# The order of SyncE's loads and stores, and wider sums of the samples' state, in a hybrid mLSTM and attention step

## The chip, the cores and the metric

The kernel runs on one core of one Trainium2 chip. The time is the device time of one launch in microseconds. The kernel before took 834.73 us, the median of three runs (834.29 to 835.82).

## The reference

One layer of a decoder with two branches, for a prompt of 1024 tokens and for eight samples of four tokens each. All numbers are 32-bit floats.

```python
h = rmsnorm(x, g_norm) * (1 + scale) + shift           # scale, shift, gate from silu(c) @ w_ada + b_ada
mq, mk, mv, mi, mf, mo, mz, aq, ak, av, az, gm, ga = split(h @ w_in)
y_m, C, n, m = mlstm(mq, mk, mv, mi, mf, mo, mz, C0, n0, m0)   # 4 heads of 128, chunks of 128
o   = sliding-window attention with sinks (8 heads, 2 key heads, window 128)
y_a = o * silu(az)
u   = sigmoid(gm) * (y_m @ w_mo) + sigmoid(ga) * (y_a @ w_ao)
y   = rmsnorm(x + gate * (u @ w_o), g_final)
```

For the samples, a head of the mLSTM starts from a given state `C0`, `n0`, `m0`:

```python
num = s @ v + w_inter * (q @ C);  dot = sum(s) + w_inter * (q @ n)
h   = num / max(|dot|, exp(-m_hat))
h   = h * rsqrt(mean(h * h) + eps) * g_mn
```

Outputs are `y` of prompt and samples, the new states `C`, `n`, `m` of both, and the last 128 keys and values.

## The kernel before

The tokens lie in the columns (1024 of the prompt and 32 of the samples), the channels in the partitions. Products in full precision are made of three products of rounded parts (a high and a low part of each operand). Weights come in tiles of 128 x 4 x 128 (`wr_...`, from a set of nine buffers), are rounded by ScalarE (`wh_...`), and VectorE takes the rest (`wl_...`). Most other tiles come from one set of 50 buffers (`ht`).

In order of time there are: the loads of the inputs, the norms and the scale and shift; the first two jobs (`ak`, `av`); jobs for the queries of the attention (`aq`) and for the first head's `mq`, `mk`, `mv`; then 18 pairs of jobs (`block_products`), each with seven products of blocks in place of eight. A product of a pair is twelve passes over 512 columns. The products of a pair are named by number: 5, 6, 2, 7, then product 1 of the next pair, then 3 and 4. At product 5 the pair calls `load()` of the next pair, which asks for its four tiles of weights. After product 2 stand small products for the samples (`smp`) of the next pair, which read all four tiles. Then follow the two output projections of the branches, and the last projection in row blocks (`foX` to `foZ`).

Between these products the attention, the heads of the mLSTM, the samples and the preparation of `w_out` run as generators ("streams"). A planner (`Side`) counts the time that the products should take (`side.now`) and decides between which products a generator's next step is emitted; a step yields how long it wants to wait until its next one. So a head (`head`) loads `hq`, `hk`, `hv`, `et`, `qw` in `load`, right behind the `U` products of `stage_b`, and uses them in `prep` a step later. `store` puts a store on a list, and it is emitted when 8 us of the planner's time are over, or when a load from the same memory comes.

All instructions then go through a scheduler that places them by the order of emission and by when its own model thinks them ready. TensorE's order is fixed to that of the emission (`in_order`). VectorE's and ScalarE's is fixed only while `V.on` and `S.on` are true: at the start, up to the line `V.on = S.on = False` behind the first two jobs, and in the last projection. SyncE's queue has no order of its own, except for loads with `late`. An edge of the kind `NoSync` orders two instructions in that plan; it makes no semaphore and no wait on the chip.

`sample_head(h)` computes the state of the samples for one head. The products with the old state are spread over four groups of 32 rows, and for every two heads `st` sums these groups with a matrix of zeros and ones (`C_S32`, 32 columns of the constants `cst`, 104 columns before their end), into rows 0 to 31 of a bank. ScalarE copies that to `sz`, it is scaled, transposed (`sty`), and multiplied by `gmn` into `gs`. This happens twice, for heads 1 and 3.

Of the kernel before, what the change touches and what calls it, by code (L numbers as in the profile page):

```python
# [15 lines left out]
ALU = mybir.AluOpType  # L16
# [8 lines left out]
NS = NB * NT  # L25
# [11 lines left out]
C_ID, C_S9, C_TRI, C_CM, C_AM, C_TS, C_CS, C_RS, C_S32, C_BM, C_S64 = 0, 128, 137, 265, 393, 649, 681, 713, 745, 777, 785  # L37
C_END = 849
# [135 lines left out]
def body(tc, a):  # L174
    nc = tc.nc
    with ExitStack() as ctx:
# [11 lines left out]
        def pb(shape, name):  # L188
            return ps.tile(shape, F32, tag="b", bufs=2, name=name)

        def po(shape, name):
            return ps.tile(shape, F32, tag="o", bufs=2, name=name)

        def ht(shape, name, dt=F32):
            return sp.tile(shape, dt, tag="half", bufs=50, name=name)

        def sm(shape, name, bufs=3, dt=F32):
            return sp.tile(shape, dt, tag=name, bufs=bufs, name=name)

        last = {}  # L200

        def no_sync(ins, others):
            for o in others:
                tc.add_manual_dep(ins, o.name, mybir.DependencyInfo(
                    mybir.DependencyClass.NoSync, mybir.DependencyReason.DATA), reason="order of the work")

        def in_order(ins, eng="PE"):
            i = getattr(ins, "ins", ins)
            no_sync(i, [last[eng]] if eng in last else [])
            last[eng] = i  # L210
# [27 lines left out]
        V, S, G = Ordered(nc.vector, "V"), Ordered(nc.scalar, "S"), Ordered(nc.gpsimd, "G")  # L238
# [8 lines left out]
        def stores(src=None):  # L247

            for e in list(due):
                if e[0] <= side.now or (src is not None and e[1].tensor is src):  # L250
                    due.remove(e)
                    issue(*e[1:])

        def dma(out, in_, late=False):
            stores(in_.tensor)
            issue(out, in_, late)

        def issue(out, in_, late=False, eng=None):
            ins = (eng or nc.sync).dma_start(out, in_)  # L259
            ins = getattr(ins, "ins", ins)  # L260
            if late:
                no_sync(ins, free)
                free.clear()
            free.append(ins)

        side = Side(stores, {"m": (2, 35.0), "a": (5,8.0), "x": (2, 0.0), "s": (1, 0.0), "g": (1, 0.0)}, 1.5)
        def mm(out, lhsT, rhs, start, stop, share=1, more=False):
            n = int(np.prod(rhs.shape[1:]))
            side.now += max(n, 250) / 2400 if rhs.dtype == F32R else max(n * 4 // share, 128) / 2400
            side.products += 1  # L270
            in_order(nc.tensor.matmul(out, lhsT, rhs, start=start, stop=stop, skip_group_check=more))  # L271

        def tr(out, in_, idn):
            side.now += 0.11
            side.products += 1
            in_order(nc.tensor.transpose(out, in_, idn))  # L276
# [38 lines left out]
        load_x(0, 0, 2, xT[0])  # L315
        small = ht([128, 512], "small")
        issue(small, a["small"])
        load_x(0, 2, KT, xT[0])
        load_x(1, 0, KT, xT[1])
        cst = cp.tile([128, C_END], F32, name="cst")  # L320
# [3 lines left out]
        ident = cst[:, C_ID:C_ID + 128]  # L324
# [4 lines left out]
        gmn, bada, gnorm = vec[:, 0:4], vec[:, 4:20], vec[:, 20:28]  # L329
# [656 lines left out]
        gs = cp.tile([128, NH, NS], F32, name="gs")  # L986
# [51 lines left out]
        def head(h):  # L1038
# [128 lines left out]
            if h == 2:  # L1167
                at["n0"], at["n1"] = (cp.tile([128, NH, NB], F32, name=n) for n in ("n0", "n1"))
                dma(at["n0"], a["state_n"])
                for i in range(NH):  # L1170
                    side.add("s", sample_head(i), "ob")
# [3 lines left out]
        def sample_head(h):  # L1175
            an, sxb, fls, wes = st["an"], st["sxb"], st["fls"], st["wes"]
            z = ht([128, 512], "sz")
# [28 lines left out]
            for b, m in zip(bs, ns_):  # L1206
                vf, vm = ht([NS, 512], f"vf{h}"), ht([96, 512], f"vm{h}", F32R)
                w = m * 129 + m % 2
# [31 lines left out]
                return  # L1240
            yield 3.0, "o"
            tot = po([128, 2, 129], f"st{h}")
            for i, (_, n4) in enumerate(tails):
                mm(tot[:NS, i], cst[:, C_S32:C_S32 + NS], n4, start=True, stop=True)
            ns = z[:NS, 0:258].rearrange("p (m e) -> p m e", e=129)
            S.copy(ns, tot[:NS])
            ssq = sm([NS, 2], "sssq", 2)
            for i in range(2):
                jk = sm([128, 128], "mjk", 2, BF16)
# [6 lines left out]
            for i in range(2):  # L1256
                V.tensor_scalar(ns[:, i, 0:128], ns[:, i, 0:128], d[:, i:i + 1], r[:, i:i + 1], op0=ALU.mult, op1=ALU.mult)
            yield 4.0, "b"
            ty = pb([128, 2, NS], f"sty{h}")
            for i, (g, _) in enumerate(tails):  # L1260
                tr(ty[:, i], ns[:, i, 0:128], ident[:NS, :NS])
                V.tensor_scalar(gs[:, g], ty[:, i], gmn[:, g:g + 1], None, op0=ALU.mult)
                samples_done.append(g)
            tails.clear()
            if h == NH - 1:
# [1108 lines left out]
```

## Time and profile before

| what | us |
|---|---|
| median of three runs | 834.73 |
| profiled execution | 832.12 |
| its span | 830.4 |
| TensorE busy | 810.4 |
| VectorE busy | 593.8 |
| ScalarE busy | 420.5 |
| GpSimd busy | 67.2 |

The profile is of one execution. Its span goes from the first instruction to the last, and the execution's time has 1.72 us more around it. Starts of products are measured and their ends are modelled, so the distance from one start to the next says more of a product's cost than its own duration. A row of the timeline has the start, the duration, engine, line, operation, the tiles written and read, the shape of the array and the sizes; in brackets stands the idle time before it and who ended it. SPq is SyncE's queue of DMA issues: a row there is the issue, and the data land later.

### The profile page before, as it was taken

What the parts mean: (1) busy time and instruction counts of PE and PEld (TensorE: products, weight loads), DVE (VectorE), ACT (ScalarE), POOL (GpSimd) and SP (SyncE); (2) the same over time, 40 slices, a digit from 0 to 9 for tenths busy, and PEclk for the clock granted to TensorE, in tenths of its full rate; (3) what the DMA queues carried; (4) which work ended last, traced back from release to release, by engine and by line L of the source; (5) the groups of instructions that cost most, each with busy time, mean ns of one, the idle gap of its engine ahead of it and who ended that gap; (6) DMA issues with size and microseconds to landing.
All of it is one profiled execution on the core that took longest, in us unless ns stands there. A gap on an engine that the chain in (4) does not pass through costs nothing. (4 is left out here: it accounts for less than half of the span.)

```text
span 830.4 us, 15038 instructions
## 1 busy us (share of the span) xinstructions
PE 810.4 (98%) x5129; PEld 669.3 (81%) x5129; DVE 593.8 (72%) x1479; ACT 420.5 (51%) x1030; POOL 67.2 (8%) x128
## 2 busy tenths in 40 slices
PE   6999999999999999999899999999999999999996
PEld 3779897888788788888788877887888789997775
DVE  4889886656656456475577785897569988974776
ACT  5664365555474564555455453544346654334343
POOL 0120000000000001000001000000002104250000
PEclk9999999999999999999999999999999999999998
DMA  9997766356436425479856345464336785643633
GB/s 334 378 357 238 184 201 213 118 150 217 143 111 189 114 85 150 140 240 286 268 188 205 120 141 155 143 203 142 103 117 196 230 288 172 212 146 122 202 109 108
DMA packets 106689, 153.96 MB, mean 185 GB/s; under 512 B 20448, under 2 KB 54368, under 8 KB 106580
## 3 DMA queue, kind: packets, MB, share of 16 engines
q1 hardware_dynamic: 100964, 142.25, 54.1%
q10 hardware_dynamic: 4176, 6.56, 2.2%
q0 software_dynamic: 1472, 4.20, 1.4%
q8 instruction: 40, 0.66, 0.3%
q14 instruction: 37, 0.30, 0.1%
HBM read 109.22 MB, written 44.75 MB: 185 GB/s over the span
## 5 line engine op out<-in xcount | busy, mean ns | idle before, releaser
L220 ACT ACTIVATE p<-p,nmx 128x256 f32<-128x256 f32 (+1 forms) x64 | 31.0, 486 | 12.4 <-DVE nmx L220 12.1
L271 PE MATMUL g_aq<-h_h,wh_aq 128*128 128x384 f32 (+1 forms) x96 | 32.2, 336 | 0.0
L271 PE MATMUL g_aq<-h_h,wl_aq 128*128 128x384 f32 (+1 forms) x96 | 30.9, 322 | 0.0
L271 PE MATMUL g_aq<-h_l,wh_aq 128*128 128x384 f32 (+1 forms) x96 | 30.8, 321 | 0.0
L271 PE MATMUL g_w_mo<-ym_l,wh_w_mo 128*128 128x384 f32 (+1 forms) x96 | 30.8, 321 | 0.0
L271 PE MATMUL g_w_mo<-ym_h,wh_w_mo 128*128 128x384 f32 (+1 forms) x96 | 30.8, 321 | 0.0
L271 PE MATMUL g_w_mo<-ym_l,wl_w_mo 128*128 128x384 f32 (+1 forms) x96 | 30.8, 321 | 0.0
L220 DVE CUSTOM_DVE_ANT_0 p<-sc,cst,sink 128x256 f32<-128x256 f32 (+1 forms) x64 | 26.2, 464 | 5.3 <-PE sc L271 5.2
L259 POOL DMA_DIRECT2D oD<-uqv x16 | 8.9, 554 | 183.2 <-ACT uqv L220 161.0
L220 DVE COPY p<-pt 128x512 f32<-128x512 f32 (+1 forms) x16 | 10.5, 657 | 13.6 <-PE pt L276 13.6
L271 PEld LDWEIGHTS g_aq<-h_h,wh_aq 128*128 128x128 f32 x96 | 18.0, 188 | 2.5 <-issue 1.5
L271 PEld LDWEIGHTS g_w_mo<-ym_l,wh_w_mo 128*128 128x128 f32 x96 | 18.0, 188 | 0.0
L271 PEld LDWEIGHTS g_aq<-h_l,wh_aq 128*128 128x128 f32 x96 | 18.1, 188 | 0.0
L271 PEld LDWEIGHTS g_w_mo<-ym_h,wh_w_mo 128*128 128x128 f32 x96 | 18.0, 188 | 0.0
L271 PE MATMUL sc<-ukv,uqv 64*128 64x256 f32 (+1 forms) x128 | 18.0, 390 | 0.0
L271 PEld LDWEIGHTS g_aq<-h_h,wl_aq 128*128 128x128 f32 x96 | 18.0, 188 | 0.0
L271 PEld LDWEIGHTS g_w_mo<-ym_l,wl_w_mo 128*128 128x128 f32 x96 | 18.0, 188 | 0.0
L220 ACT ACTIVATE p<-p,den 128x256 f32<-128x256 f32 (+1 forms) x32 | 14.5, 491 | 5.7 <-DVE den L220 5.6
L220 ACT ACTIVATE sq<-rows_h 128x512 f32<-128x512 f32 (+2 forms) x14 | 8.2, 582 | 17.8 <-issue 12.0
L220 DVE TENSOR_TENSOR et<-et,S 128x384 f32<-128x384 f32 (+1 forms) x12 | 6.1, 510 | 15.4 <-PE S L271 12.7
L271 PE MATMUL g_mq<-h_h,wh_mq 128*128 128x384 f32 (+1 forms) x48 | 16.8, 349 | 0.3 <-ACT mk L220 0.3
L276 PE MATMUL pt<-cst,p 128*128 128x128 f32 x120 | 16.4, 277 | 0.5 <-DVE mx L220 0.5
(2073 smaller groups left out, 2841.4 us busy)
## 6 DMA issues: line engine op xcount, KB each, us to landing
x<-xT SPq DMA_DIRECT2D x16, 256.0 KB, 5.6
early_h<-w_ada SPq DMA_DIRECT2D x8, 512.0 KB, 9.0
adar_ga<-w_ada SPq DMA_DIRECT2D x16, 256.0 KB, 4.0
wr_ga<-w SPq DMA_DIRECT2D x16, 256.0 KB, 2.9
wr_gm<-w SPq DMA_DIRECT2D x16, 256.0 KB, 3.6
taD<-gt SPq DMA_DIRECT2D x16, 256.0 KB, 2.2
tmD<-gt SPq DMA_DIRECT2D x16, 256.0 KB, 5.3
wor<-w_out SPq DMA_DIRECT2D x16, 256.0 KB, 5.1
```

Of the source, the lines that this page charges most:

```text
L220: ins = f(*args, **kw)
L259: ins = (eng or nc.sync).dma_start(out, in_)
L271: in_order(nc.tensor.matmul(out, lhsT, rhs, start=start, stop=stop, skip_group_check=more))
L276: in_order(nc.tensor.transpose(out, in_, idn))
```

## The change

Two edits. In `issue`, each load or store of SyncE that is emitted while the order of VectorE is not fixed gets an edge for the order behind the product that was emitted last. In `sample_head`, the sums `st` take all 104 columns of the constants from `C_S32` on, where they took 32; the copy takes the 104 rows; the two transposes take 104 rows and are both emitted ahead of the two multiplications, and their bank has room for 128 columns each. Rows and columns beyond 32 aren't used.

```diff
         def issue(out, in_, late=False, eng=None):
             ins = (eng or nc.sync).dma_start(out, in_)
             ins = getattr(ins, "ins", ins)
+            if eng is None and not V.on:
+                no_sync(ins, [last["PE"]])
             if late:
                 no_sync(ins, free)
                 free.clear()
...
             tot = po([128, 2, 129], f"st{h}")
+            w = C_END - C_S32
             for i, (_, n4) in enumerate(tails):
-                mm(tot[:NS, i], cst[:, C_S32:C_S32 + NS], n4, start=True, stop=True)
-            ns = z[:NS, 0:258].rearrange("p (m e) -> p m e", e=129)
-            S.copy(ns, tot[:NS])
+                mm(tot[:w, i], cst[:, C_S32:C_END], n4, start=True, stop=True)
+            nw = z[:, 0:258].rearrange("p (m e) -> p m e", e=129)
+            S.copy(nw[:w], tot[:w])
+            ns = nw[:NS]
...
-            ty = pb([128, 2, NS], f"sty{h}")
+            ty = pb([128, 2, 128], f"sty{h}")
+            for i in range(2):
+                tr(ty[:, i, 0:w], nw[:w, i, 0:128], ident[:w, :w])
             for i, (g, _) in enumerate(tails):
-                tr(ty[:, i], ns[:, i, 0:128], ident[:NS, :NS])
-                V.tensor_scalar(gs[:, g], ty[:, i], gmn[:, g:g + 1], None, op0=ALU.mult)
+                V.tensor_scalar(gs[:, g], ty[:, i, 0:NS], gmn[:, g:g + 1], None, op0=ALU.mult)
                 samples_done.append(g)
```

## The prediction

> **What bounds the kernel now.** I read the page first, then the waits of TensorE, then the timeline around the few places where TensorE stands still, then SyncE's own queue.
>
> ```profile
> span 830.4 us, 15038 instructions
> PE 810.4 (98%) x5129; PEld 669.3 (81%) x5129; DVE 593.8 (72%) x1479; ACT 420.5 (51%) x1030; POOL 67.2 (8%) x128
> PE xc L271 <- ACT xsq L220: 6.2, 1, 6.2
> PE S L271 <- DVE C L220: 2.3, 1, 2.3
> PE sty L276 <- DVE gs L220: 1.1, 2, 0.8
> ...
> PE bw L271 <- ACT bw L220: 0.7, 1, 0.7
> PE pt L276 <- DVE mx L220: 0.5, 1, 0.5
> PE g_mq L271 <- ACT mk L220: 0.3, 1, 0.3
> ...
> 818.00:830.40 12.40, 5.21 (x40) 4.84 (x39) 6.70 (x20) 3.00 (x9) 0.00 (x0) 0.81 0.23 85
> ```
>
> The first two lines are the page: TensorE is busy 810.4 of 830.4 us. Then come waits of TensorE: one of 6.2 us while the inputs arrive, and after that only small ones. The last line is one row of the table by stage: in the final 12.4 us TensorE works 5.2, so about 7 us are the closing chain of the last row block. Head and tail together are 13 of the 20 idle us, and the change reaches neither: its new line acts only while the flag of VectorE's ordering is off, which is from the end of the input projections of the first two jobs to the start of the final row blocks. No TensorE wait names a DMA. So in the middle the time is the sum of the products' pitches plus a few microseconds of stalls, and a change of the DMA order can only win those stalls or add new ones.
>
> **The wider state sums.** These are the fixed part. First the visit of `st`, in the timeline of TensorE, then two kinds of product without a change of array shape.
>
> ```profile
> L271 PE MATMUL st<-sz,cst x8: 273/273/298, 503.4 to 564.5; 128*32 128x129 f32 x8
> 503.05 0.39 PE L271 MATMUL bw<-t2h,wl_pgate__5971 128*128 128x512 f32 x1
> 503.37 0.63 PE L271 MATMUL st<-sz,cst 128*32 128x129 f32 x4
> ...
> 504.50 0.40 PE L271 MATMUL bw<-t2h,wl_pgate__5971 128*128 128x512 f32 x1
> ...
> 402.49 0.39 PE L271 MATMUL bw<-t2h,wl_pgate__4793 128*128 128x512 f32 x1
> 402.72 0.38 PE L271 MATMUL n<-hv,et 128*128 128x129 f32 x2
> 402.94 0.39 PE L271 MATMUL n<-C,qw 128*128 128x129 f32 x2
> 404.05 0.38 PE L276 MATMUL tk<-cst,hk 128*128 128x128 f32 x2
> 404.27 0.38 PE L276 MATMUL tv<-cst,hv 128*128 128x128 f32 x2
> ```
>
> From a start to the next start, a 512-column `bw` takes 402.72 - 402.49 = 0.23 us, two passes over 129 columns take 402.94 - 402.72 = 0.22, so 0.11 each, and two transposes take 404.27 - 404.05 = 0.22. Around `st`, 504.50 - 503.05 = 1.45 us hold the four passes of `st` and three `bw` (the one at 503.05 and two that lie between the second and third row, left out here). Less 3 x 0.23 that is 0.76 us for a visit. In the 128*128 shape, four passes at 0.11 would be 0.44. So a visit wins 0.32 us, and the first row shows eight passes in all, so there are two visits: 0.64 us. The loss is at the borders, where the array goes from 128*128 to 128*32 and back. 104 columns no longer fit into a 32-column shape, so I expect the row to say 128*128.
>
> The transposes of the sums:
>
> ```profile
> 516.14 0.39 PE L271 MATMUL bw<-h_h,wl_pgate__6128 128*128 128x512 f32 x1
> ...
> 517.04 0.24 PE L276 MATMUL sty<-cst,sz 32*128 32x32 f32 x1 [0.35 <-DVE gs L220]
> ...
> 517.78 0.39 PE L271 MATMUL bw<-h_h,wl_pgate__6128 128*128 128x512 f32 x1
> ...
> 579.00 0.39 PE L271 MATMUL by<-t3h,wl_phead_gate__6816 128*128 128x512 f32 x1
> ...
> 580.33 0.24 PE L276 MATMUL sty<-cst,sz 32*128 32x32 f32 x1 [0.77 <-DVE gs L220]
> ...
> 581.09 0.40 PE L271 MATMUL bx<-h_h,wl_phead_gate__6839 128*128 128x512 f32 x1
> ```
>
> The second transpose waits each time for VectorE's `gs`, which reads the first one out of the same bank; in the second visit VectorE has a long sum in front of it. The first visit costs 517.78 - 516.14 - 0.69 = 0.95 us, the second 581.09 - 579.00 - 0.69 = 1.40. After the change both transposes stand ahead of both reads, and have the full shape: 0.22 us a visit. That wins 0.73 + 1.18 = 1.91. The sum of this part is 2.55 us, all on TensorE, which is the bound here, so it should arrive whole.
>
> What could eat it: the weights of `st` grow from 32 to 104 columns, and the copy out of PSUM from 32 to 104 partitions.
>
> ```profile
> L271 PEld LDWEIGHTS n<-hv,et x64: 186/192/192, 236.4 to 469.2; 128*128 128x128 f32 x64
> 404.25 0.48 ACT L220 COPY et<-n 128x387 f32<-128x387 f32 x1 [3.00 <-PE n L271]
> ```
>
> A load of 128 columns is shown with 192 ns and yet its products follow each other at 0.11 us, so loads of that width are covered by the products before them; I cost the wider load at nothing, and the first load of a visit at most at 0.19 (two visits: 0.38). The Trainium skill, "TensorE: Matmul & The Clock Gate", section "LDWEIGHTS (loading the stationary operand)", speaks against this edit: it has the load's time go with the columns, columns / 1.2 ns. By it, as an estimate, eight loads would grow by 60 ns each, 0.48 us if none were covered, and the part would win 2.07. The 192 ns beside the 0.11 us here speak against that. The copy in the second row has 128 partitions and 387 columns and takes 0.48 us; the new one has 104 and 258, so it is below that, on an engine that is 51% busy, and only the small sums of the same visit follow it. I cost it at nothing too.
>
> **The order of SyncE's queue.** The added line gives each load and store a place behind the product emitted last. It is an edge for the order only; SyncE gets no wait on TensorE. ScalarE's and GpSimd's own DMAs are not touched. What moves is which DMA stands before which in one queue that stops at each unmet wait.
>
> ```profile
> 66.29 0.36 SPq L259 DMA_DIRECT2D n<-state_n  x1
> ...
> 371.01 0.33 SPq L259 DMA_DIRECT2D wr_ga<-w  x1
> ...
> 393.77 0.42 SPq L259 DMA_DIRECT2D wr_gm<-w  x1
> 394.48 1.87 SPq L259 DMA_DIRECT2D woDp<-wor  x2
> 396.45 0.39 SPq L259 DMA_DIRECT2D taD<-gt  x1
> 397.51 0.32 SPq L259 DMA_DIRECT2D hq<-qD  x1
> ...
> 397.24 0.39 PE L271 MATMUL bz<-h_h,wh_pgate__4766 128*128 128x512 f32 x1
> 397.92 0.83 PE L271 MATMUL U<-hv,hk 128*128 128x129 f32 x6
> ...
> 404.91 0.56 DVE L220 TENSOR_TENSOR et<-et,cst 128x384 f32<-128x384 f32 x1 [2.33 <-DMA tmD<-gt]
> 406.11 0.56 DVE L220 TENSOR_TENSOR qw<-qw,hq 128x384 f32<-128x384 f32 x1 [0.64 <-DMA qw<-wid]
> 406.99 0.71 PE L271 MATMUL S<-hq,hk 128*128 128x128 f32 x4 [2.33 <-DVE C L220]
> ```
>
> The first row is the plainest case: the code asks for `state_n` at the end of the third head, and SyncE issues it at 66 us. The second is the usual one: the weights of a pair are asked for at product 5 of the pair before, here the `bz` of 397.24, and the first tile was issued 26 us ahead. Stores run ahead too: `store` holds them back for 8 us of the planner's clock, yet `taD` goes at 396.45, as soon as it is ready, and stands before the head's loads (`hq`, and behind it `hk`, `hv`, `et` and `qw`), which the code asks for right behind the `U` of 397.92.
>
> This costs something in one place only. VectorE waits 2.33 us for `et` and 0.64 for `qw`; behind them in its queue stands the sum `C` that frees a bank for `S`, and TensorE idles 2.33 us. With the change, `woDp` and `taD` go behind the head's loads, since their 8 us are not over at 397.9, and `wr_gm`, whose product is earlier, stays before them. SyncE was through with `wr_gm` at 394.2, so the loads can go up to 397.51 - 394.2 = 3.3 us earlier, more than the 2.97 us that VectorE waited. I take the 2.33 us as won; the bounds are nothing (a buffer that isn't free, or VectorE placed otherwise) and 2.33.
>
> The new order also changes the plan for VectorE and ScalarE, which in this stretch are placed by readiness, and hands out buffers otherwise. For that I have no row; the stalls of this kind that the kernel has now outside `S` and `sty` are single waits like `bw` at 0.7 us, so I charge one more of 0.7, with bounds from -1.5 (`bw`, `pt` and `g_mq` of the first fence go, 0.7 + 0.5 + 0.3) to the 7.0 us of the slow rival.
>
> **Sum.** -2.55 - 2.33 + 0.7 = -4.2 us. The profiled execution took 832.12 us, its span and 1.72 us around it; it would take 827.9. The median of the runs is 834.73, 2.6 above that execution, and I keep that distance: 830.5 us. With the bounds this case reaches from 834.73 - 2.55 - 2.33 - 1.5 = 828.3 to 831.9, where most of the 2.33 us is gone again.
>
> **Rivals.** *The order is hidden.* No TensorE wait names a DMA, and the `S` stall may stay or be replaced by an equal one. Then only the sums count: 834.73 - 2.55 = 832.2. For it speaks that all other waits are under 1 us.
>
> *The weights come late (slower).* Their 26 us of lead shrink. From product 5 to the small products of the next pair, which read all four tiles, lie three products of twelve passes, 36 x 0.23 = 8.3 us, and a tile must land and be rounded before.
>
> ```profile
> wr_gm<-w SPq DMA_DIRECT2D x16, 256.0 KB, 3.6
> wr_av<-w SPq DMA_DIRECT2D x2, 256.0 KB, 9.7
> ```
>
> A median landing of 3.6 us leaves room; that of the first stage, 9.7, does not. It decides from a landing of somewhat under 8.3 us, if SyncE doesn't run ahead at all. It will run ahead by up to the 8 us of the stores, because it has no wait on TensorE. But where it stops at a buffer or a store just ahead of the weights, ScalarE and VectorE stand behind a missing tile. Priced at the one such wait that is shown, 2.33 us, in three of the 17 pairs that are loaded so: 3 x 2.33 - 2.55 = +4.4, 839.2 us.
>
> *The sums win nothing*, because the array shape is not what costs there, and the order nothing either: 834.7.
>
> **From this the numbers.** Forecast 0.40, hidden order 0.25, late weights 0.26, nothing 0.09. A measurement of this kernel can tell about 0.2%, 1.67 us, from no change: 833.06 to 836.40. Faster are the forecast and nearly all of the hidden order (0.21 of 0.25): 0.61. Within the bound lie the case of nothing and what is left of the hidden order: 0.13. Slower is the case of late weights: 0.26. The forecast's own range is 828.3 to 831.9. A range for 8 in 10 takes it in, the hidden order, the case of nothing, and the lower half of the late weights: 828.3 to 839.2.
>
> **What would show it.** Right: `st` rows of 128*128 with the next `bw` about 0.44 us later than without them; both `sty` transposes back to back and no wait for `gs`; `state_n` issued after 400 us; the head's loads before the stores of the same moment, and no wait of TensorE at `S` over 1 us. Wrong: a wait of ScalarE or VectorE on `wr` tiles of over 2 us with TensorE idle behind it; new waits of TensorE that sum to more than 2.6 us; or `st` with the same 0.76 us a visit.

## The result: 836.1 us, slower where faster was forecast

The median of the changed kernel is 836.11 us (835.10 to 837.22, 20 runs), that of the kernel before on the same chip 834.13 us (831.28 to 835.82, 20 runs): a ratio of 1.0025, 95% interval 1.0017 to 1.0033. The forecast was 830.5 us. The profiled execution of the changed kernel took 837.22 us, the longest of its 20, its span and 1.82 us around it; that of the kernel before took 832.12. So the two profiles differ by 5.1 us, and the medians by 2.0; why those distances differ is told with the ninth experiment. One execution of experiment 8, the profiled one, ran at a granted clock of 0.85 and took 899.60 us; it is left out of that experiment's figures.

Two lines of the page after the change:

```profile
span 835.4 us, 15022 instructions
PE 810.8 (97%) x5129; PEld 669.8 (80%) x5129; DVE 588.4 (70%) x1479; ACT 417.9 (50%) x1030; POOL 66.6 (8%) x128
```

The waits of TensorE (its product and line, the releaser, us in total, times, longest; `...` stands for rows that are left out):

```profile
...
PE g_w_mo L273 <- DVE wl_w_mo L220: 3.6, 4, 1.2
PE by L273 <- DVE hg1z L220: 1.5, 1, 1.5
PE sc L273 <- DMA ukv<-kD: 0.7, 1, 0.7
...
PE az L273 <- DVE ym_h L220: 0.5, 1, 0.5
PE smp L273 <- DMA wr_gm<-w: 0.5, 2, 0.2
```

TensorE is as busy as before, 810.8 us against 810.4. The waits `S` and `sty` are gone. In their place stand four waits of the memory's output projection (`g_w_mo`, the rounded low part `wl_w_mo` of the weights, made by VectorE), one for `hg1z`, one for `ym_h`, and some for data (`ukv`, `wr_gm`, and 0.5 us for `wg` in a row that is left out).

TensorE runs the same 5129 products in the same order in both kernels, so each can be set beside its twin. Where the distance between the two grows or shrinks, the time was lost or won. Up to 383 us the changed kernel falls behind by 1.6 us, in parts of 0.36 (arrival of the inputs), 0.53 (`wg`) and 0.70 (`ukv`). Then come +1.26 at `smp` (385 us), -2.50 at `S`, +0.36 at `bx` behind `gt`, -2.6 at the state sums, +2.1 in 640 to 662 us (`hg1z` and `ym_h`), and +1.02, +1.44, +1.07 and +1.08 in the memory's output projection (712 to 735 us), 4.6 in all. These steps sum to 4.8 of the 5.1 us. The wait for `wg` is no mark of the change: experiments 1 and 10, where no load has the edge, have 0.2 and 0.5 us of it. That for `ukv` stands in six of the seven kernels whose loads have the edge at that place (0.2 to 0.7 us) and in no other.

**The state sums** did what was worked out. TensorE's timeline of the changed kernel:

```profile
503.89 0.39 PE L273 MATMUL bw<-t2h,wl_pgate__5971 128*128 128x512 f32 x1
504.12 0.60 PE L273 MATMUL st<-sz,cst 128*104 128x129 f32 x4
...
505.01 0.39 PE L273 MATMUL bw<-t2h,wl_pgate__5971 128*128 128x512 f32 x1
...
516.66 0.39 PE L273 MATMUL bw<-h_h,wl_pgate__6128 128*128 128x512 f32 x1
516.89 0.34 PE L278 MATMUL sty<-cst,sz 104*128 104x104 f32 x2
...
517.55 0.40 PE L273 MATMUL bw<-h_h,wl_pgate__6128 128*128 128x512 f32 x1
...
578.46 0.39 PE L273 MATMUL by<-t3h,wl_phead_gate__6816 128*128 128x512 f32 x1
578.69 0.34 PE L278 MATMUL sty<-cst,sz 104*128 104x104 f32 x2
...
579.35 0.40 PE L273 MATMUL bx<-h_h,wl_phead_gate__6839 128*128 128x512 f32 x1
```

Counted as in the prediction (three long products of 0.23 us lie in each stretch), a visit of `st` takes 505.01 - 503.89 - 0.69 = 0.43 us instead of 0.76, and each visit of `sty` 0.20 instead of 0.95 and 1.40, with no wait between its two transposes. That is 2 x 0.33 + 0.75 + 1.20 = 2.6 us.

**The new waits.** VectorE of the changed kernel around the first of the four (in brackets: idle time before, and what ended it), and the products that wait:

```profile
711.61 0.55 DVE L220 SCALAR_TENSOR_TENSOR tgw_mo<-tgw_mo,g_w_mo 128x384 f32<-128x384 f32 x1 [0.43 <-PE g_w_mo L273]
...
713.16 0.54 DVE L220 TENSOR_TENSOR u_h<-u_h,tgw_mo 128x384 f32<-128x384 f32 x1
713.63 0.68 DVE L220 TENSOR_TENSOR wl_w_mo<-wr_w_mo,wh_w_mo 128x512 fp32r<-128x512 f32 x1
...
714.36 0.45 PE L273 MATMUL g_w_mo<-ym_l,wl_w_mo 128*128 128x384 f32 x1 [0.86 <-DVE wl_w_mo L220]
...
695.84 0.62 ACT L220 CAST wh_w_mo<-wr_w_mo 128x512 fp32r<-128x512 f32 x1 [2.95 <-PE g_w_mo L273]
```

The products that wait here are the first of the fifth job. Its weights had been there for long: ScalarE made their high part, the fifth of eight such casts, at 695.84. VectorE makes the low part only at 713.63, and before that it idles 0.43 us for a product of TensorE: the rounding stands in its queue behind a sum of the job before (`tgw_mo`, the row of 711.61), which can't start until that job's product is done. In the kernel before the same rounding stood at another place:

```profile
707.32 0.44 DVE L220 SCALAR_TENSOR_TENSOR tgw_mo<-tgw_mo,g_w_mo 128x288 f32<-128x288 f32 x1
707.68 1.73 DVE L220 TENSOR_TENSOR wl_w_mo<-wr_w_mo,wh_w_mo 128x512 fp32r<-128x512 f32 x1
```

It started at 707.68, behind the last sum of the third job, where the changed kernel has it two sums later, behind the second of the fourth, and TensorE came to its first product with it at 712.93. That is the first reading of the result: not a transfer that came late, but an instruction of VectorE that was given a later place.

### The profile page after: what moved, and what is told of

It reads as the page before. It is cut to its first block, busy times and chain, and to the rows that moved or that the text cites. A ratio compares the mean times of both kernels' runs of the same rounds, so it can differ in the third digit from the quotient of the medians.

```text
span 835.4 us, 15022 instructions
## 1 busy us (share of the span) xinstructions
PE 810.8 (97%) x5129; PEld 669.8 (80%) x5129; DVE 588.4 (70%) x1479; ACT 417.9 (50%) x1030; POOL 66.6 (8%) x128
## 4 chain that ended last, share of the span: by engine, by line
PE 81%; issue 6%; DVE 5%; DMA 5%; ACT 2%; SPq 1%; POOL 0%; DVEq 0%; POOLq 0%; ACTq 0%
PE bx L273 10%; PE bw L273 10%; PE by L273 10%; PE g_w_mo L273 5%; PE bz L273 5%; PE g_mq L273 3%; PE g_aq L273 3%; PE foW L273 3%; PE foX L273 3%; PE foY L273 2%; PE smp L273 2%; PE sc L273 2%; PE oT L273 2%; PE foZ L273 2%; PE pt L278 2%
## 5 line engine op out<-in xcount | busy, mean ns | idle before, releaser
L220 DVE SCALAR_TENSOR_TENSOR tgw_mo<-tgw_mo,g_w_mo 128x384 f32<-128x384 f32 (+1 forms) x24 | 12.2, 516 | 10.7 <-PE g_w_mo L273 10.5
```

The costliest lines, as they stand in the source:

```text
L220: ins = f(*args, **kw)
```

## Experiments

Unless something else is said, each kernel starts from the changed one, and is compared with the kernel before on the same chip (medians there: 834.72 us for the first four, 834.53 for the next four, 834.20 for the last four).

**1 and 2: each edit alone.** The first leaves out the two lines of the edge, the second has only these.

```
-            if eng is None and not V.on:
-                no_sync(ins, [last["PE"]])
```

> The wider state sums alone, SyncE's order as before. Both theories of the order say the same here: 2.5 us faster than the kernel before (1.9 from the two visits of the transposes, 0.6 from the two visits of the sums), with TensorE's wait at S of 2.3 us still there. If the sums win nothing, within 0.5 us of the kernel before.

> SyncE's order alone, the sums as before. If the two edits add up: 2.0 + 2.5 = 4.5 us slower than the kernel before, with the four waits of TensorE for wl_w_mo (3.6 us idle, 4.6 us by the starts of the products) in the memory branch's output projection. If the edits act on each other through the plan, it lies elsewhere, within 2 us of the kernel before.

The sums alone: 831.15 us (829.87 to 833.75), ratio 0.9958, interval 0.9941 to 0.9975. The edge alone: 839.04 us (838.18 to 840.55), ratio 1.0048, interval 1.0035 to 1.0060. So the whole loss is the edge's. In the profiled execution of the sums alone `S` waited 3.6 us, 1.2 more than in that of the kernel before. The edge alone has the waits for `wl_w_mo` without the wider sums:

```profile
PE g_w_mo L273 <- DVE wl_w_mo L220: 3.2, 4, 1.2
```

**3: the edge ends where the weights of the memory's output projection are first asked for.**

```
-            if eng is None and not V.on:
+            if eng is None and not V.on and edges:
...
                 if i == 2 and not nxt:
+                    edges.clear()
                     for d in range(2):
```

> Both edits, but the edges of the order end where the weights of the memory branch's output projection are first asked for. Theory A (the plan puts VectorE's rounding of these weights behind the sums of the job before, because their loads may not start earlier): the four waits for wl_w_mo go, 4.6 us less than with the change, so 2.6 us faster than the kernel before. Rival B (the loads and stores of the whole middle come later and the cost lies spread over it): at most 1 us less than with the change, so 1 to 2 us slower than the kernel before.

831.62 us (831.52 to 832.25), ratio 0.9960, interval 0.9948 to 0.9972: 4.5 us less than with the edge throughout. No wait for `wl_w_mo` is left; those of 1.5 us for `hg1z` and 0.5 for `ym_h` are there as before, so they come from edges ahead of that point.

**4: the edge only on the stores that are held for 8 us.**

```
-            if eng is None and not V.on:
+            if held and not V.on:
...
-                    issue(*e[1:])
+                    issue(*e[1:], held=True)
```

> Both edits, but only the stores that are held back for 8 us get the edge; loads and direct stores are placed as before. Theory A: the output projection is as before, the sums win 2.5 us, and the head's loads pass the stores, so that the wait at S of 2.3 us goes: 2.5 to 4.8 us faster than the kernel before. Rival C (it is the stores that come too late): slower than the kernel before by about 2 us, like the change.

829.99 us (828.79 to 830.38), ratio 0.9937, interval 0.9924 to 0.9949, and in the waits of TensorE no `S`, no `hg1z` and no `g_w_mo`; two of its own are small:

```profile
PE bx L273 <- ACT gt L220: 0.9, 1, 0.9
PE aw L273 <- ACT aw L220: 0.8, 1, 0.8
```

So the gain at `S` can be had without the losses. Stores that come too late, rival C, are out.

**5: the place of the rounding on VectorE alone.** The edges all stay. One more edge puts each sum `tgw_mo` of a job behind the rounding of the next job's weights, and SyncE's queue keeps the order of the changed kernel.

```
-            eng.tensor_tensor(lo, raw, hi.bitcast(F32), op=ALU.subtract)
+            ins = eng.tensor_tensor(lo, raw, hi.bitcast(F32), op=ALU.subtract)
+            last["lo"] = getattr(ins, "ins", ins)
...
-                V.scalar_tensor_tensor(t, t, 1.0, acc[:, :n], op0=ALU.add, op1=ALU.mult)
+                ins = V.scalar_tensor_tensor(t, t, 1.0, acc[:, :n], op0=ALU.add, op1=ALU.mult)
+                no_sync(getattr(ins, "ins", ins), [last["lo"]])
```

> Both edits, and one thing more: in the memory's output projection the first VectorE sum of a job (tgw_mo) is placed behind the rounding of the next job's weights (wl_w_mo), so that the rounding no longer stands behind the last sum of the job before. SyncE's own order is that of the changed kernel. Theory A (the place of the rounding on VectorE is the cost, its data has long landed): the four TensorE waits g_w_mo <- VectorE wl_w_mo, 4.6 us by the trace, go: 836.1 - 4.6 = 831.5, between 830.5 and 832.5; the waits hg1z 1.5 and wr_gm stay. Rival B (SyncE asks for the weights too late: 714.3 and 718.2 us in the changed kernel against 709.4 and 713.3 before): VectorE then stands in front of the sums waiting for the weights, TensorE waits for the same time under another name (tgw_mo or wh_w_mo), and the time stays within 1 us of 836.

831.87 us (830.71 to 833.53, 12 runs), ratio 0.9971, interval 0.9959 to 0.9983. The median is 4.2 us below that of the changed kernel, by a place on VectorE alone; the trace had 4.6 at these waits. Two of the waits of TensorE beyond those of the kernel before (`ym_h` with 0.5, `ukv` with 0.4 and `bx` behind `gt` with 0.2 us are there too):

```profile
PE by L273 <- DVE hg1z L220: 1.5, 1, 1.5
...
PE smp L273 <- DMA wr_gm<-w: 0.2, 1, 0.2
```

VectorE's timeline at the rounding that was shown above:

```profile
707.52 1.78 DVE L220 TENSOR_TENSOR wl_w_mo<-wr_w_mo,wh_w_mo 128x512 fp32r<-128x512 f32 x1
709.22 0.54 DVE L220 SCALAR_TENSOR_TENSOR tgw_mo<-tgw_mo,g_w_mo 128x384 f32<-128x384 f32 x1
```

The rounding is back at 707.52, no product waits for it, and nothing waits for the weights instead. The rival, weights that are asked for too late, is out.

**6: which edges gave it that place.** The edge is left out on the loads of that stage's gates (`tgw_mo`) and of the output weights' parts (`woD`); SyncE's order is again that of the changed kernel.

```
-            if eng is None and not V.on:
+            if eng is None and not V.on and not skip:
...
+            skip.append(0)
             gated(JOBS_OUT[JOBS_OUT.index(n) + 1])
+            skip.clear()
...
+                skip.append(0)
                 dma(raw, woD[n, k], True)
+                skip.clear()
```

> Both edits, the edge left out only on two groups of loads in the last stage: the gates of the memory's output projection (tgw_mo) and the parts of the output weights (woD). SyncE's queue holds the same order as in the changed kernel; only the plan differs, and with it VectorE's order: five of the seven roundings wl_w_mo stand one sum or more earlier. Theory A (these edges move the sums and roundings in the plan, and the place on VectorE is the cost): three or four of the four waits go, 831.5 to 832.7. Rival B (the loads come late on SyncE, whatever VectorE's order): stays within 1 us of 836.

833.07 us (832.72 to 834.49, 12 runs), ratio 0.9989, interval 0.9978 to 1.0000. Three of the four waits for `wl_w_mo` go, one of 0.8 us stays. The time is 0.4 us above the expected range, and 1.2 above experiment 5. Neither group of loads feeds the rounding. They feed the sums and the parts that share VectorE with it.

**7: the complement of 4, the edge on all but the held stores.**

```
-            if eng is None and not V.on:
+            if eng is None and not held and not V.on:
```

> Both edits, the edge only on the loads and stores that are issued at once, not on the stores held for 8 us: the complement of the run with the edge on held stores only, which took 829.99. Theory A (the cost in the new plan comes from the edge on loads, the gain of the S wait from the edge on held stores): the waits wl_w_mo (4.6), hg1z and ym_h (2.1) and wr_gm (1.2) are all there and the S wait of 2.3 to 3.6 us stays too: 831.15 + 7.9 = 839.1, between 837 and 841. Rival B (loads without held stores cost little; only both together do): 831 to 833.

841.74 us (840.39 to 842.55), ratio 1.0092, interval 1.0072 to 1.0111, 0.7 us above the range of theory A, and not by its sum. The waits of TensorE:

```profile
PE g_w_mo L273 <- DVE wl_w_mo L220: 3.5, 4, 1.2
PE smp L273 <- DMA wr_ga<-w: 1.6, 2, 1.4
PE by L273 <- DVE hg1z L220: 1.5, 1, 1.5
PE g_mq L273 <- ACT aq L220: 0.9, 1, 0.9
```

All the losses are there, `smp` is dearer, and there are new ones early on. Behind the wait at `smp` the granted clock fell, which no term of the expectation had (a row of the table by stretches has its bounds and length, busy time and records of each engine from TensorE on, then the granted clock, the share of the DMA engines, GB/s):

```profile
385.50:388.30 2.80, 1.08 (x7) 0.44 (x5) 0.59 (x1) 1.24 (x3) 0.00 (x0) 1.00 1.06 382
388.40:391.70 3.30, 3.29 (x32) 2.34 (x33) 3.30 (x8) 2.58 (x8) 0.00 (x0) 0.50 0.66 253
```

By the twins the stretch from 383 to 400 us costs 4.6 us here, and 1.25 in the changed kernel. But the wait at `S`, which theory A let stay, is gone here too. VectorE's timeline:

```profile
410.74 0.35 DVE L220 SCALAR_TENSOR_TENSOR C<-C,dec,U 128x129 f32<-128x129 f32 x1
412.26 0.56 DVE L220 TENSOR_TENSOR et<-et,cst 128x384 f32<-128x384 f32 x1 [1.17 <-DMA et<-nmd]
```

`C` stands ahead of `et` here. So that order, and the gain at `S` with it, doesn't need an edge on the held stores.

**8 and 10: which held stores.** The eighth has the edge only on the output weights' stores (`woD`), the tenth only on the gates' (`taD`, `tmD`).

```
-            if eng is None and not V.on:
+            if held and any(out.tensor is k for k in kept) and not V.on:
```

> Both edits, the edge only on the held stores of the output weights' parts (woD), not on those of the gates (taD, tmD) and the attention's and memory's outputs. If it is these 256 KB stores ahead of head 1's loads at 391 to 399 us that made S wait, the S wait goes as with all held stores, and the waits bx <- gt (0.9) and aw (0.6) of that run go as well if they come from the other held stores: 828.5 to 830. If it is the gates' stores, S still waits 2 to 3.6 us: 831 to 832.5.

> Both edits, the edge only on the held stores of the gates' blocks (taD, tmD): the complement of the run with the edge on the output weights' stores only, which took 832.77. If the gates' stores ahead of head 2's loads made S wait, the S wait goes and the time is 829 to 830.5, like 829.99 with all held stores; if each of the two groups brings a part, S waits 1 to 2 us and the time is 830.5 to 832; if neither alone moves it, 831 to 833.

The eighth took 832.55 us in the median (831.01 to 834.98, 11 runs; 832.77 with the one that is left out), ratio 0.9982, interval 0.9967 to 0.9996: near the case that was expected if `S` still waits (831 to 832.5). The tenth took 829.64 us (829.06 to 833.23), ratio 0.9951, interval 0.9934 to 0.9967. That is the time expected if the gates' stores were what kept `S` waiting, and yet `S` is among the waits of TensorE:

```profile
PE S L274 <- DVE C L220: 1.8, 1, 1.8
```

VectorE's timeline says why:

```profile
404.74 0.56 DVE L220 TENSOR_TENSOR et<-et,cst 128x384 f32<-128x384 f32 x1 [1.96 <-DMA et<-nmd]
406.16 0.34 DVE L220 SCALAR_TENSOR_TENSOR C<-C,dec,U 128x129 f32<-128x129 f32 x1
```

VectorE still has `et`, whose load came late, ahead of `C`, and by the twins `S` starts only 0.6 us earlier, not 2.5. Most of the gain over the sums' 2.6 us must lie elsewhere; what experiment 9 says of the clock is the likely place, but that isn't shown. In the eighth kernel VectorE's order, which is laid before the kernel runs, is the same in this (only the order of these rows is read):

```profile
437.24 0.56 DVE L220 TENSOR_TENSOR et<-et,cst 128x384 f32<-128x384 f32 x1 [1.70 <-DMA et<-nmd]
437.71 0.34 DVE L220 SCALAR_TENSOR_TENSOR C<-C,dec,U 128x129 f32<-128x129 f32 x1
```

So neither group alone moves `C`; the edge on all held stores does (experiments 4 and 11), and so does the edge on everything else (experiment 7).

**9: TensorE kept busy in the wait of `S`.** The sums alone, and nine products of ones into unused columns.

```
+                for _ in range(9 if (h, p) == (2, 2) else 0):
+                    in_order(nc.tensor.matmul(bank[:, 384:512], one, one, start=True, stop=True))
```

> The sums edit alone, and nine products of ones (128x128 of f32, into 128 unused columns of tk's bank; extra work whose result is not used) between tv's transposes and S of head 2's last group, where TensorE waits 2.3 to 3.6 us for C. Theory A (after 3.6 us of idle the granted clock is 0.50 for 5.3 us, which costs some 2.4 us more than the wait itself): with the idle filled the clock stays 1.00 in 408 to 414 us, the time falls from 831.15 to 829 to 830 and the spread of the runs (829.87 to 833.75) shrinks to about 1 us, though TensorE has nine products more. Rival B (the wait's length and the runs' spread have another cause): the products take their 2 us inside the wait, the time stays at 831.15 or rises, and the spread stays at 4 us.

830.32 us (829.09 to 831.41), ratio 0.9949, interval 0.9936 to 0.9963, against 831.15 (829.87 to 833.75) without the products, each compared with runs of the kernel before on its own chip. The median is 0.3 us above the expected range, the spread is 2.3 us instead of 3.9; the two intervals overlap, so the 0.8 us between the medians isn't clear of noise, and the clock in the traces has to decide. The stretches around `S` in the table by stretches, first without and then with the extra products:

```profile
404.00:406.50 2.50, 0.68 (x7) 0.44 (x5) 0.40 (x1) 1.73 (x8) 0.10 (x1) 1.00 0.76 245
406.80:408.20 1.40, 0.00 (x0) 0.00 (x0) 0.82 (x2) 0.00 (x0) 0.00 (x0) 0.50 0.98 371
...
410.00:413.50 3.50, 3.50 (x9) 2.65 (x9) 1.80 (x3) 1.70 (x5) 0.00 (x0) 0.50 0.70 224
```

```profile
408.00:413.50 5.50, 5.50 (x56) 4.54 (x55) 3.46 (x6) 3.37 (x8) 0.00 (x0) 1.00 0.68 235
```

In the execution without them `S` waited 3.55 us, the granted clock fell to 0.50 within that wait, and the products behind it ran at 0.50. TensorE's timeline of that execution, the same last product in the kernel before, and that kernel's row of the table by stretch:

```profile
408.23 1.22 PE L271 MATMUL S<-hq,hk 128*128 128x128 f32 x4 [3.55 <-DVE C L220]
...
413.51 0.42 PE L271 MATMUL bx<-h_l,wh_pgate__4824 128*128 128x512 f32 x1
```

```profile
409.84 0.39 PE L271 MATMUL bx<-h_l,wh_pgate__4824 128*128 128x512 f32 x1
```

```profile
408.20:413.50 5.30, 5.30 (x53) 4.30 (x51) 3.62 (x6) 2.91 (x8) 0.00 (x0) 1.00 0.74 249
```

From `S` to that `bx` it is 413.51 - 408.23 = 5.28 us here and 409.84 - 406.99 = 2.85 there, 2.4 us more for the same products. The wait was 2.33 us in the profiled execution of the kernel before, and its clock stayed at 1.00. Of the other executions only the mean granted clock is known. In experiment 1 the profiled execution has 0.993 (833.29 us), one more has 0.993 (833.75), and the other four have 0.997 to 0.999 and took 829.87 to 831.73. The profiled execution of the kernel before, whose clock stayed at 1.00 here, has 0.997; of its 57 executions that were timed beside the experiments 43 have 0.996 or less, and of the 20 of the changed kernel none. So most executions of the kernel before lose some clock that the changed kernel keeps. That they lose it at `S` is argued, not shown: the mean doesn't say where. It would explain the 2.0 us by which the median of the kernel before lies above its profiled execution; the other 1.1 of the 3.1 us between the two distances are the changed kernel's, whose profiled execution is its longest.

**11: held stores, and only until the attention's output projection begins.**

```
-            if eng is None and not V.on:
+            if held and edges and not V.on:
...
             yield
+            edges.clear()
             jobs[0].load()
```

> Both edits, the edge on held stores only, and only until the attention's output projection begins. The S wait stays away, and the two waits of 645 to 660 us that the run with all held stores had (aw <- ScalarE aw 0.57 longer, ay <- VectorE yat4l 0.43) go, if they come from the stores behind that point: 829.99 - 1.0 = 829.0, between 828.3 and 829.6. If they come from the plan ahead of it, 829.6 to 830.4.

828.41 us (828.14 to 829.57), ratio 0.9930, interval 0.9917 to 0.9942: the fastest of all, 7.7 us below the changed kernel. Beyond what the kernel before has, TensorE's waits show one, of 0.4 us at `by` for ScalarE.

**12: the pair weights without the edge.**

```
+                        skip.append(n)
                         dma(t, a["w1"][JOBS[n]][:, 4 * kh:4 * kh + 4])
+                        skip.clear()
```

> Both edits, the edge on everything but the loads of the block products' pair weights (wr_). Theory A (that edge lets the pair weights come late, 1.26 us at smp at 385 us): that wait goes, 836.11 - 1.26 = 834.85, between 834 and 835.5; the waits wl_w_mo, hg1z and ym_h stay. Rival B (the weights, asked for earlier, go ahead of head 2's loads): the S wait is back, 2.3 to 3.6 us, and the time is 837 to 839.

834.69 us (834.22 to 835.28, 11 runs), ratio 1.0006, interval 0.9997 to 1.0015: 1.4 us less than the changed kernel. By the twins the 1.25 us at `smp` are back, and 0.65 of the first wait for `wl_w_mo` too. `S` didn't come back; of the waits for `wl_w_mo` 3.0 us of idle time are still there, where the changed kernel has 3.6.

## Why the prediction was wrong

**The sums: right.** 2.55 us were worked out, the trace has 2.6, and the shape reads 128*104 where I expected 128*128. Alone they bring 834.72 to 831.15, and the interval of that ratio (2.1 to 4.9 us) holds 2.6. The wider weight load cost nothing that can be seen: a load of `st` shows 168 ns for 104 columns, and a visit costs 0.43 us, as its four passes at 0.11 do. This is where a rule of the Trainium skill was weighed ("TensorE: Matmul & The Clock Gate", section "LDWEIGHTS (loading the stationary operand)"): it would have made the gain 2.07, and the visits speak against counting the load.

**The wait at `S`: right in size, wrong in cause.** I let the head's loads go up to 3.3 us earlier. The sum `C` in the kernel before, behind `et` and `qw`:

```profile
406.59 0.34 DVE L220 SCALAR_TENSOR_TENSOR C<-C,dec,U 128x129 f32<-128x129 f32 x1
```

SyncE and VectorE of the changed kernel:

```profile
401.61 0.33 SPq L259 DMA_DIRECT2D hq<-qD  x1
...
406.91 0.32 SPq L259 DMA_DIRECT2D et<-nmd  x1
...
408.65 0.38 SPq L259 DMA_DIRECT2D taD<-gt  x1
...
406.90 0.34 DVE L220 SCALAR_TENSOR_TENSOR C<-C,dec,U 128x129 f32<-128x129 f32 x1
...
409.89 0.56 DVE L220 TENSOR_TENSOR et<-et,cst 128x384 f32<-128x384 f32 x1 [0.82 <-DMA et<-nmd]
```

The head's loads do stand ahead of the gates' store `taD` now, as written. But that of `et` is issued at 406.91, and `S` starts at 407.32 without a wait: a load asked for 0.4 us ahead can't be what helped it. What changed is VectorE's queue: `C`, which frees the bank for `S`, stood behind `et` and `qw` and now stands ahead of them. The other traces agree: in the kernel before and in experiments 1, 9 and 10 `C` stands behind `et`, and `S` waits 1.0 to 3.6 us; in the changed kernel and in experiments 2 to 7, 11 and 12 it stands ahead, and `S` waits 0.4 us at most. So the 2.33 us of the sum came true by luck: the order that brought them is one that the prediction named only as a way to lose them.

**The new plan of VectorE and ScalarE: the step that failed.** I wrote that for it "I have no row" and charged one stall of 0.7 us. It cost 4.6 in the memory's output projection (experiments 3 and 5), 2.1 for `hg1z` and `ym_h`, 1.3 at `smp` (experiment 12), and 0.4 at `bx` behind `gt`: 8.4 us, more than the upper bound of 7.0 too. The wait for `ukv` comes on top, with 0.7 us in the profiled execution; it was not tried by itself. I treated the edge as a change of SyncE's queue with a small side effect on the rest. It is the other way round. Both the gain at `S` and the loss at `g_w_mo` are changes of VectorE's order. The way from the edge to that order is argued: a load that is placed later in the plan makes every instruction that reads it ready later there, and VectorE's order in this stretch is laid by readiness. Experiment 6 fits it, since there SyncE's order is kept and VectorE's changes; the planner's own times are in no trace. The place where `hg1z` went was not tried by itself; in the kernel before it starts at 641.53, in the changed one it stands behind roundings of the attention's weights (`wl_ao`), of which the last is shown:

```profile
643.19 0.42 DVE L220 TENSOR_TENSOR wl_ao0C<-wr_ao,wh_ao0C 128x256 fp32r<-128x256 f32 x1
643.53 0.68 DVE L220 TENSOR_TENSOR hg1z<-p,by 128x512 f32<-128x512 f32 x1
```

The prediction could have seen the danger: it quoted VectorE's `et` ahead of `C`, an order that costs 2.33 us, `U` of 397.92 being long done, and still priced a new order at 0.7.

**The distance from profile to median: a term without a row.** The sum added the 2.6 us by which the kernel before's median lay above its profiled execution, and kept them for the changed kernel. There the median lies 1.1 us below. The mean clock is 0.997 or more in all 20 executions of the changed kernel, and not in most of those of the kernel before (experiment 9): a gain that the sum didn't have. So the medians show less of the miss than the profiles do.

**The rivals.** The late weights did happen, in one pair and for about 1.3 us, not in three for 2.33 each; the number of the slower case was too high, and its mechanism is a seventh of the loss. "The order is hidden" and "nothing" are out.

**The signs.** SyncE's issue of `state_n` (duration, first and last start):

```profile
L259 SPq DMA_DIRECT2D n<-state_n x1: 429/429/429, 440.3 to 440.3; - x1
```

It comes at 440.3 us, after 400 as written; the visits of `st` and `sty` have the length that was written, and `S` has no wait. Of the signs for wrong, the second came: new waits of TensorE of over 2.6 us in all. The first, ScalarE or VectorE waiting for `wr` tiles, is not what stands before `g_w_mo`.

## What to carry to other kernels

- An edge "for the order only" on a DMA is here also an edge in the plan of every engine whose work is laid by readiness. Before pricing it, list the instructions that share an in-order queue with the readers of that DMA, and ask which of them TensorE needs soon: an instruction whose data has long landed is lost by standing behind one whose data has not.
- When such a change costs, pin the few instructions that matter (experiment 5 gave back 4.2 us by the place of one kind of rounding) or limit the edge to where it gains (experiment 11, 828.41 us).
- A gain of the expected size doesn't show that the expected cause brought it: look whether the load it was put down to really went earlier.

## What was not expected of the hardware

A TensorE wait of 3.55 us was followed by a granted clock of 0.50 for some 5 us, which cost 2.4 us besides the wait; the wait of 2.33 us at the same place in the kernel before was not. With nine products in the gap, which left 1.0 us of waiting, the clock stayed at 1.00. So where this wait grew from 2.33 to 3.55 us it cost 1.2 and 2.4 more, and the prediction had no such term.

These rows give no safe length for a wait. In experiment 1 TensorE fell idle at 408.23 - 3.55 = 404.68, and the clock stood at 0.50 from 406.8 on, some 2 us later. In experiment 7 it stood at 0.50 from 388.4 to 391.7 though no single wait there was over 1.4 us: in the 2.8 us before, TensorE was busy for 1.08. The Trainium skill ("TensorE: Matmul & The Clock Gate", "Part 1: The HAM clock gate") has the clock halve after an idle window of about 3.4 us. The waits of 3.55 and 2.33 us would fit that; the fall within the first of them and the row of experiment 7 don't, and there the measurement decides.
